# The order of every engine's instructions made by a second timing model, in a two-layer hybrid decoder trunk

## The chip, the cores and the metric

The kernel runs on one core of one Trainium2 chip. The metric is the device time of one launch, in microseconds (us). Engines are called as in the profile: PE is TensorE's matmul row, PEld its weight loads, DVE is VectorE, ACT is ScalarE, POOL is GpSimd, SP is SyncE, which issues all DMAs here.

## The reference

The reference computes two decoder layers on 256 rows of 1024 floats. Each layer norms its input, projects it, runs two groups of heads on the projection and puts their gated outputs through one output projection:

```python
for layer in range(DEPTH):
    h = rmsnorm(x, pre_norm[layer])
    proj = h @ w_in[layer]
    (hq, hf, hi, hz, nq, kc, vc, ks, vs, kw, vw, ng, nz) = jnp.split(proj, offsets, axis=-1)
    o_h = hgrn2_mixer(heads(hq), heads(hf), heads(hi), lower_bounds[layer].reshape(HGRN_HEADS, HEAD_DIM))
    o_h = rmsnorm(o_h, hgrn_out_norm[layer]).reshape(B, S, HGRN_WIDTH) * jax.nn.silu(hz)
    o_n = nsa_mixer(heads(nq), heads(kc), heads(vc), heads(ks), heads(vs), heads(kw), heads(vw), ng, ...)
    o_n = o_n.reshape(B, S, NSA_WIDTH) * jax.nn.silu(nz)
    y = jnp.concatenate([o_h, o_n], axis=-1).astype(x.dtype) @ w_out[layer]
    x = x + rmsnorm(y, post_norm[layer]).astype(x.dtype)
```

`hgrn2_mixer` is a gated linear recurrence with 8 heads of 128 by 128 state. `nsa_mixer` is attention with 8 query heads and three branches (compressed blocks, selected blocks, a sliding window), mixed by sigmoid gates. Everything is float32.

## The kernel before, in words

**Matmuls.** A float32 product is made of three products of parts: each operand is split into a high part of type fp32r and the rest. The normed input stands in SBUF as Hhi and Hlo for the whole layer. Projections are done in two shapes: `mm_a` (L363, matmuls L368 to L370) with the input stationary and 512 weight columns moving, and `mm_b` (L373, L378 to L380) with the weights stationary and 256 rows moving. The output projection is `mm_o` (L995, L997 to L999).

**Weights.** The list `plan` (L182) holds all weight units of both layers, 168 of them. `Ring.fill` (L206) issues their DMAs on SP into five raw buffers; `Ring.convert` (L199) splits each: ACT casts the high part (L202, whi) and DVE subtracts it for the low part (L203, wlo), into eight buffers each. A unit's buffers are given back when the matmuls that read it are done (`done`, L240).

**Planned order.** The kernel is traced in an order that its author writes by hand with a small clock: `tick` (L126) counts matmul time, `later` (L122) puts a piece of work some us behind, and `flush` (L131) forces it out. Transposes, rope, softmax steps, scans and conversions come between the projections' matmuls in this way. `norm_in` (L335) is the input norm: squares and sums on ACT (L339), a sum on DVE (L341), the root on ACT and its reciprocal on DVE (L331, L332), the scaling on DVE (L344), then `turn_h`: transposes on PE (L351) and their copies into Hhi on ACT (L355) and Hlo on DVE (L356). `finish` (L1002) is the post-norm of half of the rows, of the same kind (L1008 on ACT, L1009, L1010 and L1014 on DVE, and L331 and L332), and calls `norm_in` for the second layer. At the seam of the layers the chain is: last matmul of a half, L1008, L1009, L1010, L331, L332, L1014, L339, L341, L331, L332, L344, L351, L355, first L368.

**Attention.** For each half of the rows and each of two key groups: scores (L608 to L610), maximum and exp (L627 on DVE, L630 on ACT), coefficients and scaling (L640 to L651 on DVE), transposes (L668) with copies (L670 on ACT, L671 on DVE), values (L686 to L688), and a copy of the result (L691 on ACT). The compressed keys are roped at L386 to L393 and transposed at L531 (tile kst).

**Gates.** `hz` (L963) takes the gate projection from PSUM with a SiLU (L974) and multiplies (L978); `nz` (L439) does the same for attention (L450, L453). PSUM is shared out in banks: three with the tag mm for projections, two s, two t, one o.

**The framework's part.** What the kernel writes is not the final order. On leaving the TileContext, the framework runs the traced program through a timing model. Whenever an engine can take an instruction, the scheduler gives it, among those whose operands and buffers are ready in the model, the one that was traced first. So the traced order is a preference, and the model decides what is passed over. It then places the semaphores for the order that came out. On the chip each engine runs its instructions in that fixed order. This goes for PE, ACT, DVE, POOL and for SP's DMA issues, and also fixes which buffer of a pool a tile gets. A second, general path (`layers(True)`, L1120) is in the program behind a branch that is not taken with these inputs.

## Time and profile before

| | us |
|---|---|
| median of 3 runs | 566.41 |
| lowest and highest run | 566.41 and 568.52 |
| the profiled execution, its own time | 566.25 |
| its span, from the first to the last instruction | 564.5 |
| PE busy | 548.2 (97%) |
| DVE busy | 398.0 (71%) |
| ACT busy | 332.2 (59%) |
| mean granted clock of TensorE, as a share of full speed | 0.994 |

The profile is of one execution. Its span is 1.75 us shorter than the time of that execution; that part lies around the span. Busy time is the union of an engine's instructions. Matmuls are pipelined and overlap, so that a matmul's own duration (0.40 us for 512 columns) is longer than the distance to the next one. A row of a timeline gives the start in us from the span's start, the duration, engine, line, operation, output and inputs, shapes and number of instructions; in brackets stands how long the engine was idle before it and what ended that.

### The profile page before, as it was taken

What the parts mean: (1) busy time and instruction counts of PE and PEld (TensorE: products, weight loads), DVE (VectorE), ACT (ScalarE), POOL (GpSimd) and SP (SyncE); (2) the same over time, 40 slices, a digit from 0 to 9 for tenths busy, and PEclk for the clock granted to TensorE, in tenths of its full rate; (3) what the DMA queues carried; (4) which work ended last, traced back from release to release, by engine and by line L of the source; (5) the groups of instructions that cost most, each with busy time, mean ns of one, the idle gap of its engine ahead of it and who ended that gap; (6) DMA issues with size and microseconds to landing.
All of it is one profiled execution on the core that took longest, in us unless ns stands there. A gap on an engine that the chain in (4) does not pass through costs nothing. (4 is left out here: it accounts for less than half of the span.)

```text
span 564.5 us, 9581 instructions
## 1 busy us (share of the span) xinstructions
PE 548.2 (97%) x3563; PEld 490.3 (87%) x3563; DVE 398.0 (71%) x880; ACT 332.2 (59%) x626; POOL 9.6 (2%) x18
## 2 busy tenths in 40 slices
PE   7999999999999999999989999999999999999993
PEld 4889998999888989988878999879988898998882
DVE  4897997889577277663678599878967654866422
ACT  6577447855366785552557763686626768746310
POOL 4000000000000001001000000000000000000000
PEclk9999999999999999999999999999999999999997
DMA  8697559953146058565475755698423622856111
GB/s 302 204 315 236 150 149 280 302 175 114 38 126 194 21 186 291 162 214 151 133 240 170 230 151 157 197 303 257 117 72 82 170 87 70 301 172 202 40 38 43
DMA packets 72196, 96.55 MB, mean 171 GB/s; under 512 B 3383, under 2 KB 49229, under 8 KB 72142
## 3 DMA queue, kind: packets, MB, share of 16 engines
q1 hardware_dynamic: 72142, 95.86, 55.3%
q8 instruction: 30, 0.49, 0.3%
q14 instruction: 24, 0.20, 0.1%
HBM read 93.75 MB, written 2.10 MB: 170 GB/s over the span
## 5 line engine op out<-in xcount | busy, mean ns | idle before, releaser
L203 DVE TENSOR_TENSOR wlo<-raw,whi 128x1024 fp32r<-128x1024 f32 (+1 forms) x168 | 202.8, 1222 | 60.4 <-ACT whi L202 57.4
L202 ACT CAST whi<-raw 128x1024 fp32r<-128x1024 f32 (+1 forms) x168 | 175.0, 1052 | 89.0 <-PE ps_mm L379 24.4
L378 PE MATMUL ps_mm<-Hhi,whi 128*128 128x256 f32 x448 | 127.5, 285 | 0.0
L379 PE MATMUL ps_mm<-Hlo,whi 128*128 128x256 f32 x448 | 125.7, 281 | 0.0
L380 PE MATMUL ps_mm<-Hhi,wlo 128*128 128x256 f32 x448 | 125.7, 280 | 0.0
L368 PE MATMUL ps_mm<-whi,Hhi 128*128 128x512 f32 (+1 forms) x256 | 101.5, 397 | 2.3 <-ACT Hhi L355 2.3
L369 PE MATMUL ps_mm<-wlo,Hhi 128*128 128x512 f32 (+1 forms) x256 | 98.9, 386 | 0.0
L370 PE MATMUL ps_mm<-whi,Hlo 128*128 128x512 f32 (+1 forms) x256 | 98.8, 387 | 0.0
L379 PEld LDWEIGHTS ps_mm<-Hlo,whi 128*128 128x128 f32 x448 | 84.5, 189 | 0.1
L378 PEld LDWEIGHTS ps_mm<-Hhi,whi 128*128 128x128 f32 x448 | 84.3, 188 | 0.1
L380 PEld LDWEIGHTS ps_mm<-Hhi,wlo 128*128 128x128 f32 x448 | 84.4, 188 | 0.0
L368 PEld LDWEIGHTS ps_mm<-whi,Hhi 128*128 128x128 f32 x256 | 48.9, 191 | 10.2 <-ACT Hhi L355 3.0
L370 PEld LDWEIGHTS ps_mm<-whi,Hlo 128*128 128x128 f32 x256 | 48.6, 190 | 10.2 <-DVE Hlo L356 0.3
L369 PEld LDWEIGHTS ps_mm<-wlo,Hhi 128*128 128x128 f32 x256 | 48.8, 191 | 7.6 <-DVE wlo L203 0.5
L627 DVE CUSTOM_DVE_ANT_0 ps_s<-ps_s,cm 128x128 f32<-128x128 f32 (+1 forms) x64 | 22.4, 370 | 2.1 <-PE ps_s L610 0.7
L630 ACT ACTIVATE sB<-ps_s,nm 128x256 f32<-128x256 f32 (+1 forms) x40 | 16.9, 430 | 10.8 <-DVE nm L627 10.1
L671 DVE TENSOR_TENSOR sB<-ps_t,sB 128x512 fp32r<-128x512 f32 x12 | 8.2, 687 | 20.1 <-ACT sB L670 20.1
L1009 DVE TENSOR_TENSOR sA<-ps_mm,sB 128x512 f32<-128x512 f32 x6 | 4.2, 692 | 21.6 <-ACT st L1008 21.6
L997 PE MATMUL ps_mm<-whi,sN 128*128 128x512 f32 x48 | 19.0, 396 | 0.0
L998 PE MATMUL ps_mm<-wlo,Hhi 128*128 128x512 f32 x48 | 19.0, 395 | 0.0
L999 PE MATMUL ps_mm<-whi,Hlo 128*128 128x512 f32 x48 | 18.9, 395 | 0.0
L999 PE MATMUL ps_mm<-whi,sN 128*128 128x512 f32 x48 | 18.9, 394 | 0.0
(282 smaller groups left out, 927.7 us busy)
## 6 DMA issues: line engine op xcount, KB each, us to landing
raw<-in_w_in SPq DMA_DIRECT2D x112, 512.0 KB, 4.6
raw<-in_w_out SPq DMA_DIRECT2D x32, 512.0 KB, 4.3
raw<-in_w_in SPq DMA_DIRECT2D x8, 536.0 KB, 4.7
raw<-in_cmp_w_k SPq DMA_DIRECT2D x16, 256.0 KB, 3.3
raw<-in_cmp_w_v SPq DMA_DIRECT2D x16, 256.0 KB, 3.3
sB<-in_x SPq DMA_DIRECT2D x3, 512.0 KB, 3.5
sB<-in_post_norm SPq DMA_DIRECT2D x2, 512.0 KB, 5.4
xs<-sB SPq DMA_DIRECT2D x4, 256.0 KB
```

What stands on the lines that cost most here:

```text
L202: S.copy(out=hi, in_=raw)
L203: V.tensor_tensor(out=lo, in0=raw, in1=hi.bitcast(F32), op=OP.subtract)
L368: P.matmul(out=ps, lhsT=hh, rhs=wh, start=k == 0, stop=False)
L369: P.matmul(out=ps, lhsT=hh, rhs=wl, start=False, stop=False)
L370: P.matmul(out=ps, lhsT=hl, rhs=wh, start=False, stop=k == KT - 1)
L378: P.matmul(out=ps, lhsT=wh, rhs=hh, start=k == 0, stop=False)
L379: P.matmul(out=ps, lhsT=wh, rhs=hl, start=False, stop=False)
L380: P.matmul(out=ps, lhsT=wl, rhs=hh, start=False, stop=k == KT - 1)
L627: V.tensor_tensor_reduce(out=sb[b], in0=sb[b], in1=mk[b], scale=-1.0, scalar=3e38, op0=OP.add, op1=OP.min, accum_out=nm[:, i, b:b + 1])
L997: P.matmul(out=ps, lhsT=hi, rhs=wh, start=first, stop=False)
L998: P.matmul(out=ps, lhsT=hi, rhs=wl, start=False, stop=False)
L999: P.matmul(out=ps, lhsT=lo, rhs=wh, start=False, stop=last)
```

## The change

The context is told to use the framework's other timing model for the scheduling, a timeline simulation, instead of the default. No line of the computation changes, and the traced order stays as it was. The kernel has no other place that reads the flag.

```diff
-    with tile.TileContext(nc) as tc, ExitStack() as ctx:
+    with tile.TileContext(nc, schedule_with_timeline_sim=True) as tc, ExitStack() as ctx:
         build(ctx, tc, A, out)
```

## Rows read from the trace of the kernel before

**Rows 1.** Part 1 of the page: busy us, share of the span, instructions.

```profile
PE 548.2 (97%) x3563; PEld 490.3 (87%) x3563; DVE 398.0 (71%) x880; ACT 332.2 (59%) x626; POOL 9.6 (2%) x18
```

**Rows 2.** Waits of TensorE: line waited for, us in total, times, longest us.

```profile
PE ps_mm L1056 <- DMA sB<-in_pre_norm: 2.4, 1, 2.4
PE ps_mm L368 <- ACT Hhi L355: 2.3, 2, 1.8
PE ps_t L531 <- DVE kst L393: 1.3, 1, 1.3
PE ps_t L351 <- DVE sA L344: 1.0, 1, 1.0
```

**Rows 3.** Windows: stretch, busy us of PE, PEld, DVE, ACT, POOL; clock, DMA.

```profile
14.11:280.00 265.89, 265.80 (x1757) 239.84 (x1756) 195.84 (x440) 161.64 (x300) 3.67 (x3) 1.00 0.59 181
285.00:551.00 266.00, 264.73 (x1754) 239.05 (x1753) 189.24 (x420) 157.49 (x302) 0.00 (x0) 1.00 0.52 158
```

**Rows 4.** Timeline of PE, seam: start us, us, line, op, tiles, shape, idle before.

```profile
282.28 0.60 PE L351 MATMUL ps_t<-ct,sA 128*128 128x128 f32 x4
284.68 0.50 PE L368 MATMUL ps_mm<-whi,Hhi 128*128 128x512 f32 x1 [1.80 <-ACT Hhi L355]
...
285.71 0.40 PE L370 MATMUL ps_mm<-whi,Hlo 128*128 128x512 f32 x1
```

**Rows 5.** Timeline of DVE in the same stretch.

```profile
272.21 0.15 DVE L1010 TENSOR_TENSOR yss<-yss 128x1 f32<-128x1 f32 x1
273.30 1.23 DVE L203 TENSOR_TENSOR wlo<-raw,whi 128x1024 fp32r<-128x1024 f32 x1 [0.94 <-ACT whi L202]
274.45 0.16 DVE L332 RECIPROCAL r<-r 128x1 f32<-128x1 f32 x1
...
279.52 1.21 DVE L203 TENSOR_TENSOR wlo<-raw,whi 128x1024 fp32r<-128x1024 f32 x1
280.65 1.41 DVE L344 SCALAR_TENSOR_TENSOR sA<-sB,r,sB 128x512 f32<-128x512 f32 x2
```

**Rows 6.** Timeline of ACT in the same stretch.

```profile
273.18 0.29 ACT L331 ACTIVATE r<-yss,eps_t 128x1 f32<-128x1 f32 x1
...
282.52 1.04 ACT L202 CAST whi<-raw 128x1024 fp32r<-128x1024 f32 x1 [2.19 <-DMA raw<-in_w_in]
...
284.05 1.07 ACT L355 CAST Hhi<-ps_t 128x512 fp32r<-128x512 f32 x2
```

**Rows 7.** Part 5 of the page: weight split; busy us, mean ns, idle us before.

```profile
L203 DVE TENSOR_TENSOR wlo<-raw,whi 128x1024 fp32r<-128x1024 f32 (+1 forms) x168 | 202.8, 1222 | 60.4 <-ACT whi L202 57.4
L202 ACT CAST whi<-raw 128x1024 fp32r<-128x1024 f32 (+1 forms) x168 | 175.0, 1052 | 89.0 <-PE ps_mm L379 24.4
```

**Rows 8.** Timelines of DVE and PE, end of the first layer's attention.

```profile
204.66 0.69 DVE L671 TENSOR_TENSOR sB<-ps_t,sB 128x512 fp32r<-128x512 f32 x1
...
205.48 0.28 PE L686 MATMUL ps_o<-sB,vhi 128*128 128x256 f32 x1
```

**Rows 9.** Timeline of DVE before kst is ready, second layer.

```profile
371.59 3.50 DVE L203 TENSOR_TENSOR wlo<-raw,whi 128x1024 fp32r<-128x1024 f32 x3 [0.53 <-ACT whi L202]
...
375.44 0.21 DVE L393 TENSOR_TENSOR kst<-kst,rt 15x64 f32<-15x64 f32 x1
```

**Rows 10.** Waits of ACT for weight loads: us in total, times, longest us.

```profile
ACT whi L202 <- DMA raw<-in_w_in: 10.0, 10, 2.2
```

**Rows 11.** Timelines of ACT at a table load and of PE at the kernel's start.

```profile
197.01 1.28 ACT L943 ACT_TABLE_LOAD   x1
198.31 0.31 ACT L943 ACTIVATE hr<-hss,eps_t 128x16 f32<-128x16 f32 x1
...
12.43 0.63 PE L370 MATMUL ps_mm<-whi,Hlo 128*128 128x512 f32 x1
```

**Rows 12.** Timelines of ACT and PE: a bank emptied, and the group that takes it.

```profile
200.89 0.62 ACT L974 ACTIVATE sA<-ps_mm 128x512 f32<-128x512 f32 x1
...
207.94 0.48 PE L368 MATMUL ps_mm<-whi,Hhi 128*128 128x512 f32 x1
```

## Prediction

> **What bounds the kernel now.** I read four views in this order: the busy table, the waits of TensorE, the windows, and the timelines of the few places where TensorE stops. The busy table [rows 1] has TensorE at 548.2 of 564.5 us. The instructions stay what they are under the change, so only the remaining 16.3 us and the order can move. The waits [rows 2] name 7.0 us of those: 2.4 us before the first matmul (the first load), 1.0 us for the first norm, 2.3 us in front of L368 for Hhi, and 1.3 us in front of L531 for kst. The other 9.3 us are the tail after the last matmul. The windows [rows 3] say that the two long stretches between are full: 265.80 of 265.89 us and 264.73 of 266.00 us busy, at a granted clock of 1.00, the 2.4 GHz level. ScalarE and VectorE are busy 161.64 and 195.84 us in the first of them: they are not the bound, but everything that TensorE eats goes through them.
>
> So **a better order can gain only what stands in these waits**, and a worse one can lose as much as it takes away from the lead that ScalarE and VectorE have over TensorE.
>
> **Where the lead is thick.** The weights are split by L202 and L203, 168 times, 1052 and 1222 ns each [rows 7]. A ring holds 8 split units. 168 units feed 532 us of matmuls (the two stretches of [rows 3]), so one unit is 3.2 us of TensorE work and a full ring about 25 us. A conversion that is issued one or two places later is hidden by that stock. If the ring ran empty, each one would cost its 1.22 us.
>
> **Where it is thin: the seam of the two layers.** The last matmuls of the first layer are followed by L351 (transposes of the normed rows), L355 and the first L368 of the second layer. L351 starts its last group at 282.28 us and L368 follows at 284.68, after 1.80 us of idle [rows 4]. The chain to L351 changes engine at each step, and in each step it stands behind weight conversions. Sums of squares are added at 272.21 us (done 272.36), the root L331 starts at 273.18 on ScalarE [rows 5, 6], 0.8 us later. The reciprocal follows at 274.45, behind the conversion of 273.30: the root was done at 273.47, so 1.0 us more. L344 starts at 280.65, when the conversion of 279.52 is through. And L355, whose transposes were there at about 282.9 us, comes at 284.05, behind a conversion of 282.52: 1.1 us [rows 4, 6]. These delays are some 4 us, and part of them is hidden by the matmuls of the other half; 1.8 us reach TensorE. This is also the place that shows that the order is the framework's: the first L370 stands at 285.71, 1.03 us behind the first L368 and so some four matmuls later, where the program has it third of its group.
>
> **Thin hand-offs in attention.** The last VALUE step waits for L671: it runs from 204.66 to 205.35 us and L686 starts at 205.48, a lead of 0.13 us [rows 8]. And kst: its last step L393 came at 375.44 us, because three conversions from 371.59 on stood ahead of the rope [rows 9]; that is the 1.3 us of [rows 2].
>
> **The change part by part.** It removes and adds no operation. It moves any of them by the second model's opinion of what is ready. (1) TensorE's own order: matmuls cost the same at any place, so 0 by itself, if operands are there. (2) ScalarE and VectorE at the seam. The chain has six changes of engine. Bounds: −1.8 us (all conversions behind the chain) and +6.8 us (one conversion more at each of six, 6 × (1.05 + 1.22)/2). I take two more, one on each engine: 1.05 + 1.22 = +2.3 us, since at that place TensorE already waits and nothing covers them; two, because conversions become ready there about once per freed unit, as the six changes against one conversion each now show. (3) The hand-offs with 0.13 us of lead: a conversion ahead costs 1.22 − 0.13 = 1.1 us. Four places (two attention ends in each layer), bounds 0 and 4.4; I take two, +2.2 us. (4) kst: −1.3 us to +1.3 us (the first layer gets what the second has); I take 0. (5) DMA issues on SP: the weight loads stay in the order of the list, small loads can move past them. ScalarE waits for a weight load 10 times now, 2.2 us at most [rows 10]; the ring covers that, 0, with −0.5 to +2.2 as ends. POOL's memsets run far ahead of their readers: 0. (6) Table loads of ScalarE. One takes 1.28 us: it starts at 197.01 and its activation, the next instruction, at 198.31 [rows 11]. A new order of sigmoid, silu, exp and root could add some, between 0 and 1.3 us each; I take 0, since ScalarE idles for 40% of the time and none stands in the seam's chain. The Trainium skill (ScalarE: Activation LUTs, What ACT_TABLE_LOAD costs) counts a drain of about 1.38 us on top, 2.66 us per switch. The trace does not agree: the activation follows the load by 0.02 us [rows 11]. By the page, one extra switch in a chain would be 2.7 us and the sum would be 573.4 us.
>
> **The sum** is made against the profiled execution, 566.25 us (span 564.5 and 1.75 around it), which lies 0.16 us under the median of the runs, 566.41. 566.25 + 2.3 + 2.2 = 570.75, say **570.8 us**, 0.8% slower. A difference of about 0.5% (2.8 us) is what a measurement of this kernel can tell from no change; the three runs lie 0.4% apart.
>
> **Rivals.** *No change that can be told.* The second model is ready with nearly the same opinions, or gives the very same order; swaps stay inside the ring's 25 us and the seam stays as it is. For it: 97% busy, and the ring's stock. Against it: the seam and the four thin hand-offs have no cover at all. Time 566.2 to 568. Chance 0.33.
>
> *Faster: the seam and kst close.* If the second model sees the conversions become ready later than the norm's steps, L331, L332, L344 and L355 go ahead of them, and kst ahead of its three. Price: −1.8 − 1.3 = −3.1 us, 563.1 us. It decides when at most one of the six changes at the seam meets a conversion. For it: 4 us of conversions stand in that chain now, so there is something to take out. Against it: it needs both places, since either alone is below 0.5%. Nothing larger is to be had, as [rows 2, 3] show. Chance 0.21.
>
> *Much slower: the gate's PSUM banks come free late.* Projections rotate over three banks (tag "mm"). In the gate stage a bank is emptied by the SiLU L974, which stands behind squares, root and two table loads on ScalarE; it empties the second of two at 200.89 to 201.51 us, and the next group, which needs one of them, starts at 207.94 [rows 12], a lead of at least 6.4 us. It decides from there: if the new order puts over 6.4 us of ready conversions and copies ahead of that chain, TensorE stops, since it issues in order. A slip of 10 us (eight or nine conversions) gives 3.6 us in each layer, 7.2 in all, on top of the forecast: 578.0 us. For it: an order by readiness has no notion of a chain that is late. Against it: 6.4 us is a long way, and ScalarE idles 40% of the time. Chance 0.10.
>
> What a longer stop could cost besides: a 512-column matmul at the start of the kernel takes 0.63 us [rows 11], after the seam 0.40 [rows 4]. So the 1.80 us of the seam did not take the clock to its lower level, and a stop of that size costs nothing beyond itself here. The Trainium skill (TensorE: Matmul & The Clock Gate, Part 1) says that an idle array falls back to 1.2 GHz and has to be busy again before it gets 2.4 GHz. No row here shows that inside the kernel; by it a stop much longer than the seam's would add 0.23 us to each of some matmuls behind it: 2.3 us for ten, 573.1 us in all, inside the range.
>
> **How the numbers follow.** Forecast 0.36, much slower 0.10, no change 0.33, faster 0.21. Faster by over 0.5%: 0.21. Within: 0.33. Slower: 0.36 + 0.10 = 0.46. Cases of both signs hold much of the chance, so the forecast's own range is 568.5 (one of the items) to 577 (all of (2) and (3)). The range for all is 562.5 to 580: below it lies the end of the faster case (about 0.10), above it the longer slips of the much slower one (about 0.08).
>
> **What would show it.** Right: the wait of L368 for Hhi at the seam grows from 1.8 to about 4 us, with L331, L332 or L355 directly behind L202 or L203; new waits of TensorE of about 1 us in front of L686 or L668 behind L671 and L651. No change: the same four waits within 0.5 us. Faster: the waits in front of L368 and L531 are gone and no others appear. Much slower: waits of several us in front of L368 in the gate stage, near 208 and 481 us, for L974. I am wrong altogether if TensorE's busy time itself grows while its waits don't, or if the head (before the first L368) or the tail moves by more than 1 us: there I count nothing, since the head is the first load and the tail a chain of data without conversions.

## The result and the profile after

The changed kernel takes **583.18 us** (median of 4 runs, 582.66 to 585.32) against 566.41 us for the kernel before: a ratio of 1.0287, 95% interval 1.0253 to 1.0322. It is 16.8 us slower, above the range that was forecast (562.5 to 580.0). The profiled execution has a span of 580.9 us, 16.4 more than before. The busy table of its page, which answers to [rows 1]:

```profile
PE 553.8 (95%) x3563; PEld 493.5 (85%) x3563; DVE 398.7 (69%) x880; ACT 333.6 (57%) x626; POOL 9.6 (2%) x18
```

The instructions are the same in number on every engine. TensorE's busy time grew by 5.6 us and its idle time by 10.8. The waits of TensorE (line waited for, us in total, times, longest us), which answer to [rows 2]:

```profile
PE ps_mm L368 <- ACT sA L974: 5.7, 2, 2.8
PE ps_t L351 <- DVE sA L344: 3.3, 2, 2.3
PE ps_mm L1056 <- DMA sB<-in_pre_norm: 2.3, 1, 2.3
PE ps_s L853 <- ACT sB L630: 1.6, 2, 0.8
PE ps_o L681 <- ACT pcT L659: 1.5, 2, 0.8
PE ps_mm L368 <- ACT Hhi L355: 1.2, 2, 0.7
PE ps_s L608 <- ACT sB L630: 1.0, 2, 0.5
PE ps_s L934 <- ACT sB L630: 0.7, 2, 0.4
```

The largest is new: TensorE stops in front of L368 for L974, the gate's SiLU, once in each layer. The wait for kst is gone. Four small waits on the softmax's ScalarE steps (L630, L659) are new.

The next two fences show one source line each over 110 to 250 us (the first layer): first of the kernel before, then of the changed one. The two times behind the colon are the first and the last start.

```profile
L608 PE MATMUL ps_s<-kTh,q x24: 279/291/392, 113.3 to 180.5; 128*128 128x272 f32 x16, 128*128 128x256 f32 x8
L934 PE MATMUL ps_s<-sA,ATt x32: 271/275/275, 183.1 to 194.3; 128*128 128x128 f32 x32
L974 ACT ACTIVATE sA<-ps_mm x4: 594/600/616, 199.9 to 214.3; 128x512 f32<-128x512 f32 x4
```

```profile
L608 PE MATMUL ps_s<-kTh,q x24: 279/287/384, 112.8 to 196.5; 128*128 128x272 f32 x16, 128*128 128x256 f32 x8
L934 PE MATMUL ps_s<-sA,ATt x32: 275/275/377, 197.4 to 203.5; 128*128 128x128 f32 x32
L974 ACT ACTIVATE sA<-ps_mm x4: 589/596/601, 210.5 to 221.0; 128x512 f32<-128x512 f32 x4
```

The scores (L608) begin within 0.5 us of each other, and the last one starts 16.0 us later. The last mix (L934) starts 9.2 us later, the first SiLU 10.6 us later. What fills TensorE in between can be read from windows of 10 us (columns as in [rows 3]). First two of the kernel before, then the same two of the changed one and the two where it pays:

```profile
120.00:130.00 10.00, 10.00 (x82) 9.81 (x83) 9.73 (x37) 5.36 (x16) 0.00 (x0) 1.00 0.34 104
130.00:140.00 10.00, 10.00 (x85) 9.48 (x84) 9.40 (x27) 6.16 (x17) 0.00 (x0) 1.00 0.55 158
```

```profile
120.00:130.00 10.00, 10.00 (x86) 10.00 (x85) 9.55 (x34) 5.04 (x14) 0.00 (x0) 1.00 0.69 195
130.00:140.00 10.00, 10.00 (x54) 8.41 (x53) 6.81 (x17) 4.60 (x11) 0.00 (x0) 1.00 0.42 123
200.00:210.00 10.00, 7.61 (x66) 7.13 (x64) 4.22 (x13) 9.92 (x38) 0.00 (x0) 1.00 0.19 59
210.00:220.00 10.00, 8.82 (x40) 7.40 (x41) 6.99 (x16) 6.48 (x10) 0.00 (x0) 0.83 0.27 77
```

From 130 to 140 us TensorE is full in both kernels, but with 54 instructions instead of 85: long projections in place of short attention steps. Nothing is lost there. The bill comes at 200: the projections that can go ahead are through, three banks are full, and only the late, dependent steps are left. Now ScalarE is the engine that is full (9.92 of 10), and then the granted clock falls to 0.83. The stop itself, on ScalarE and on TensorE (timelines):

```profile
207.01 0.59 ACT L670 CAST sB<-ps_t 128x512 fp32r<-128x512 f32 x1
207.62 1.28 ACT L943 ACT_TABLE_LOAD   x1
208.91 0.31 ACT L943 ACTIVATE hr<-hss,eps_t 128x16 f32<-128x16 f32 x1
209.24 1.28 ACT L974 ACT_TABLE_LOAD   x1
210.53 1.09 ACT L974 ACTIVATE sA<-ps_mm 128x512 f32<-128x512 f32 x2
```

```profile
211.18 0.50 PE L368 MATMUL ps_mm<-whi,Hhi 128*128 128x512 f32 x1 [2.83 <-ACT sA L974]
211.52 0.39 PE L369 MATMUL ps_mm<-wlo,Hhi 128*128 128x512 f32 x1
...
212.38 0.63 PE L369 MATMUL ps_mm<-wlo,Hhi 128*128 128x512 f32 x1
212.81 0.63 PE L370 MATMUL ps_mm<-whi,Hlo 128*128 128x512 f32 x1
```

The matmul of 512 columns takes 0.63 us at the 1.2 GHz level and 0.39 us at 2.4, and starts follow at 0.43 and 0.23 us. In the first layer 8 starts from 211.99 to 215.37 us stand at the lower level (3.38 us where 8 × 0.233 = 1.87 would do), in the second 14 from 492.75 to 498.83 (6.08 instead of 3.27): 1.5 + 2.8 = 4.3 us. They count as busy, so most of TensorE's 5.6 us of added busy time is the same work at half speed.

**The account of the profiled execution**: stops 2 × 2.83 = 5.7, half speed 4.3, the four small waits of attention 4.8, the seam +1.6 (idle 2.28 + 0.47 + 0.68 = 3.4 us against 1.80), kst −1.3. Together 15.1 of 16.4 us.

### The profile page after: what moved, and what is told of

Read it like the earlier page. It is cut to its first block, busy times and chain, and to the rows that moved or that the text cites. A ratio compares the mean times of both kernels' runs of the same rounds, so it can differ in the third digit from the quotient of the medians.

```text
span 580.9 us, 9606 instructions
## 1 busy us (share of the span) xinstructions
PE 553.8 (95%) x3563; PEld 493.5 (85%) x3563; DVE 398.7 (69%) x880; ACT 333.6 (57%) x626; POOL 9.6 (2%) x18
## 5 line engine op out<-in xcount | busy, mean ns | idle before, releaser
L203 DVE TENSOR_TENSOR wlo<-raw,whi 128x1024 fp32r<-128x1024 f32 (+1 forms) x168 | 203.6, 1223 | 81.6 <-ACT whi L202 78.1
L368 PE MATMUL ps_mm<-whi,Hhi 128*128 128x512 f32 (+1 forms) x256 | 101.9, 398 | 6.9 <-ACT sA L974 5.7
L370 PE MATMUL ps_mm<-whi,Hlo 128*128 128x512 f32 (+1 forms) x256 | 100.1, 392 | 0.7 <-DVE Hlo L356 0.7
L369 PE MATMUL ps_mm<-wlo,Hhi 128*128 128x512 f32 (+1 forms) x256 | 100.4, 393 | 0.0
L368 PEld LDWEIGHTS ps_mm<-whi,Hhi 128*128 128x128 f32 x256 | 49.6, 194 | 17.1 <-ACT sA L974 6.1
L370 PEld LDWEIGHTS ps_mm<-whi,Hlo 128*128 128x128 f32 x256 | 49.7, 194 | 10.5 <-DVE Hlo L356 1.4
L630 ACT ACTIVATE sB<-ps_s,nm 128x256 f32<-128x256 f32 (+1 forms) x40 | 17.1, 430 | 25.1 <-DVE nm L627 17.1
L997 PE MATMUL ps_mm<-whi,sN 128*128 128x512 f32 x48 | 19.0, 395 | 0.0
L998 PE MATMUL ps_mm<-wlo,sN 128*128 128x512 f32 x48 | 18.9, 394 | 0.0
L999 PE MATMUL ps_mm<-whi,Hlo 128*128 128x512 f32 x48 | 18.7, 396 | 0.0
L997 PE MATMUL ps_mm<-whi,Hhi 128*128 128x512 f32 x48 | 18.6, 395 | 0.0
L630 ACT ACTIVATE sN<-ps_s,nm 128x128 f32<-128x128 f32 (+1 forms) x24 | 9.4, 400 | 15.9 <-DVE nm L627 13.5
```

What stands on the lines that cost most here:

```text
L203: V.tensor_tensor(out=lo, in0=raw, in1=hi.bitcast(F32), op=OP.subtract)
L368: P.matmul(out=ps, lhsT=hh, rhs=wh, start=k == 0, stop=False)
L369: P.matmul(out=ps, lhsT=hh, rhs=wl, start=False, stop=False)
L370: P.matmul(out=ps, lhsT=hl, rhs=wh, start=False, stop=k == KT - 1)
L630: S.activation(out=Pm[i][:, b, :], in_=sb[b], func=AF.Exp, bias=nm[:, i, b:b + 1], scale=-1.0, accum_out=sm[:, i, 1 + b:2 + b])
L997: P.matmul(out=ps, lhsT=hi, rhs=wh, start=first, stop=False)
```

## The experiments

The order that a model makes can be taken out of it and tied to the instructions of the other: an edge from each instruction of an engine to the next, which sets the order of issue and makes nothing wait for a result. The model then only orders what is left free, and it orders that anew, around the tied engine. All orders below are stored as runs of positions in the listed program. Line numbers in these kernels are shifted by the lists. In the first model's order 281 of TensorE's 3417 instructions stand elsewhere than in the list, in the second model's 1509.

```diff
+    def put_in_order(engine, runs):
+        seq = [i for i in nc.cur_bb.bb.instructions if i.engine == engine ...]
+        seq = [seq[s + k] for s, n in runs for k in range(n)]
+        for p, i in zip(seq, seq[1:]):
+            tc.add_manual_dep(i, p.name, mybir.DependencyInfo(mybir.DependencyClass.NoSync,
+                              mybir.DependencyReason.DATA), reason="order")
...
     layers(False)
+    put_in_order(mybir.EngineType.PE, RUNS)
```

### TensorE's order against all the others

The kernel before, with TensorE in the second model's order (the edit above, RUNS from the changed kernel):

> The first model schedules, but TensorE's 3417 matmuls and transposes are tied in the order that the second model gave them; ScalarE, VectorE and the queues stay with the first model. Theory A (the 16.8 us come from TensorE's own order: projections issued ahead of attention, then a stop for the gate's PSUM banks): 580 to 585 us, with the two stops of about 3 us in front of L368 for L974. Theory B (they come from the orders of ScalarE and VectorE, conversions ahead of the softmax): 566 to 571 us.

Measured: 581.37 us, ratio 1.0261 [1.0233, 1.0288]. TensorE waits 5.8 us in front of the gate's projections for the SiLU, as in the changed kernel. The changed kernel, with TensorE in the first model's order:

> The second model schedules, but TensorE's 3417 instructions are tied in the order that the first model gave them. Theory A: 564 to 569 us, no wait of L368 for L974 over 0.5 us, and the kst wait may stay closed (then nearer to 564). Theory B: 579 to 584 us.

Measured: 583.61 us, ratio 1.0329 [1.0290, 1.0368]. **Each theory was right in one run and wrong in the other.** Tying the second model's order of TensorE to the kernel before costs 15.2 us, and tying the first model's to the changed kernel leaves 17.5, where the flag costs 16.8. In the second run there is no stop for the gate; the time goes in small waits inside attention and in 3.0 us at the seam. Its VectorE and TensorE, timelines (the conversion L203 is L217 here, the scaling L651 is L665, the transposes L668 are L682):

```profile
125.70 0.22 DVE L650 TENSOR_TENSOR pc<-pc,cm 128x64 f32<-128x64 f32 x1
126.46 1.23 DVE L217 TENSOR_TENSOR wlo<-raw,whi 128x1024 fp32r<-128x1024 f32 x1 [0.54 <-ACT whi L216]
...
129.35 1.22 DVE L217 TENSOR_TENSOR wlo<-raw,whi 128x1024 fp32r<-128x1024 f32 x1
...
131.09 0.87 DVE L665 TENSOR_SCALAR sN<-sN,sm 128x128 f32<-128x128 f32 x4
```

```profile
131.43 0.94 PE L682 MATMUL ps_t<-ct,sN 128*128 128x128 f32 x4 [1.50 <-DVE sN L665]
```

Two conversions stand between the steps of one softmax, where the kernel before has one, in a stretch where VectorE is full (9.41 us of 120 to 130), and TensorE waits for the result. In the changed kernel TensorE has projections in that stretch (the windows above).

These two runs don't split the loss into halves, since the free engines follow the tied one. By the places of the same instructions in the traces, VectorE's stand in the first run 1.5 places on average from the changed kernel's order and 3.8 from the order before, ScalarE's 0.3 and 3.9; in the second run it is the other way round, with 2.2 places from the order before and 3.6 from the changed kernel's on VectorE, 0.4 and 3.9 on ScalarE. So the first run shows that TensorE's order, with what the first model then does to the others, is enough for the stops and for most of the loss. The second shows that moves on VectorE and ScalarE that are small by comparison cost as much when TensorE keeps the first model's order.

**The listed order.** Two runs tied TensorE in the order of the list, under the second and under the first model (the edit is the one above with the runs left out):

> The second model schedules, TensorE's instructions are tied in the order in which the program lists them. In the first model's order 281 of 3417 stand elsewhere than in the list, in the second's 1509. Theory A: 564 to 570 us, near the tied order of the first model. Theory B: 579 to 584 us.

> Control of the run before: the first model, TensorE's instructions tied in the listed order. Theory A: 565 to 570 us, within 2 us of the same order under the second model. Theory B: also 565 to 570 us, but 10 us or more below the second model with the same order. If the few moves that the first model makes on TensorE are worth something, this one is slower than the kernel before by what they are worth.

Measured: 610.78 us (1.0789 [1.0759, 1.0819]) and 598.81 us (1.0574 [1.0546, 1.0601]). The times that both theories named were far off. The 281 moves of the first model are worth 33 us: without them TensorE waits 17.2 us for L344 and 7.9 us for a constant's load (prow). The idea that the first model's order is good because it is near the list was wrong; few moves in the right places make it good.

### Which of the other engines

A ladder down from the second run above: TensorE tied in the first model's order, and one engine more tied at each step.

> The second model, with TensorE's and VectorE's instructions tied in the first model's orders; 81 of ScalarE's instructions and 26 of SP's loads stand elsewhere than before. Theory C (VectorE's order is the other half: the weights' second conversions L203 stand ahead of softmax steps and wait there for ScalarE's first half, with the softmax queued behind them): 564 to 569 us. Rival S (ScalarE's or SP's moves cost it): 575 us or more.

> The second model with TensorE, VectorE and ScalarE all tied in the first model's orders; 26 of SP's 215 loads and two memsets of GpSimd still stand elsewhere. Against the run with TensorE and VectorE tied (576.3 us) only ScalarE's 81 places are new. If those 81 places cost the 10.5 us that were left: 565 to 569 us. If SP's loads cost them: 574 to 578 us.

> The second model with TensorE, VectorE, ScalarE and also SP's 215 loads tied in the first model's orders; two memsets of GpSimd change places and the order in which semaphores are numbered differs. If order is all that the flag changes, and the 4.8 us left were SP's loads: 564 to 567 us. If the 4.8 us come from anything else: about 570 us.

Measured: 576.28 us (1.0187 [1.0142, 1.0233]), 570.23 us (1.0090 [1.0071, 1.0109]), 566.16 us (0.9995 [0.9970, 1.0020]). Each set of runs has its own times of the kernel before; above these the four runs of the ladder lie by 17.5, 10.5, 4.8 and 0.4 us. So, with TensorE's order kept, VectorE's costs 7.0 us, ScalarE's 81 displaced instructions 5.7, SP's 26 displaced loads 4.4, each to within some 2 to 3 us by the intervals, and nothing is left: **order is all that the flag changes.** Theory C, which had VectorE alone as the other half, was wrong in its "564 to 569"; the run of 570 us lies between its two expectations. What SP's order costs shows in part in the waits of TensorE in the run of 570 us: it waits 2.0 us for prow (a constant, loaded in two parts of 32 KB), and for kst in both layers (1.3 us of that stand in the kernel before too):

```profile
PE ps_t L623 <- DVE kst L485: 2.1, 2, 1.5
PE ps_t L385 <- DMA prow<-in_cmp_pos_v: 2.0, 1, 2.0
```

Between the profiles of these last two runs (spans 568.5 and 563.2 us) TensorE's idle time differs by 2.8 us and its busy time by 2.5. Part of the latter are matmuls at the lower clock behind the wait for prow (the last section has the rows).

Two mixtures left TensorE and ScalarE free and tied VectorE alone:

> The first model, with VectorE alone tied in the second model's order; TensorE and ScalarE are ordered freely around it (TensorE then stands 4.4 places per instruction from the second model's order and 11.3 from the first's). Theory C: 578 to 585 us, and the stop of L368 for L974 comes back. Rival (VectorE's order hurts only where TensorE's is held fast, as in the second run of the first set): 566 to 571 us.

> The second model, with VectorE alone tied in the first model's order; TensorE and ScalarE are ordered freely. Theory C with VectorE as the root: 564 to 571 us. Rival (TensorE's order of the second model is bad by itself, whatever VectorE does): 578 to 585 us, with the stop for L974.

Measured: 599.75 us (1.0574 [1.0535, 1.0614]) and 593.95 us (1.0480 [1.0433, 1.0528]). Both are worse than either kernel and lie above every time that was expected. The second was expected at 564 to 571 if VectorE were the root: it is not. In these two runs a model that is forced to one engine's order of the other model makes a worse whole than either model does alone.

### Where in the program

The first model's orders on TensorE, VectorE and ScalarE, tied only for what is listed from the start of attention to the end of the second gate, and the counterpart with everything else tied:

```diff
+            mark()
             flush("q")
             attention(PW, PS)
...
             nz(ring)
+            mark()
```

> The second model, with the first model's orders on TensorE, VectorE and ScalarE only for what is listed from the start of attention to the end of the second gate, in both layers; head, first projections, keys, output projection and seam are free. Theory L (the loss is made in that stage: the first output projection comes 7.0 us late, the seam adds 1.4, the second layer 8.2): 566 to 571 us, with no wait for L974. Rival (the orders of the stages are bound to each other, and a cut between two models costs waits of its own): 575 us or more.

> The counterpart: first model's orders for everything outside that stage, the second model inside it. Theory L: 579 to 585 us, with the two stops of about 3 us in front of L368 for L974. Rival: no more than half of the loss, 566 to 575 us.

Measured: 569.60 us (1.0078 [1.0053, 1.0104]) and 584.81 us (1.0359 [1.0332, 1.0387]). Theory L holds: the stage from attention to the gates, left to the second model, costs all of it; with that stage put right 4.2 us are left above the kernel before of the same set (565.45 us), so 12.6 of 16.8 us are back. The rest lies mainly at the seam, where this run waits longest, and with it the clock (timeline of TensorE; the matmuls behind the wait take 0.63 us again):

```profile
285.61 1.32 PE L450 MATMUL ps_t<-ct,sA 128*128 128x128 f32 x8 [3.28 <-DVE sA L443]
287.41 0.63 PE L467 MATMUL ps_mm<-whi,Hhi 128*128 128x512 f32 x1 [0.48 <-ACT Hhi L454]
287.84 0.63 PE L468 MATMUL ps_mm<-wlo,Hhi 128*128 128x512 f32 x1
```

### The stop at the gate: cause or symptom

First, only what is listed while the gate's projections are listed is held to its place of the first order, on TensorE alone:

```diff
+            mark()
             hz(l, ring, rs)
+            mark()
```

> The second model, with only TensorE's instructions listed while the gate's projections are listed (in hz) each held behind the instruction that stands ahead of it in the first model's order; ScalarE and VectorE are free, and so is the rest of TensorE. Theory G (the gate's projections run ahead, fill the three banks, and TensorE then has nothing but dependent steps until L974): the stop goes, and with it the half-speed matmuls behind it, 568 to 575 us. Rival (attention is late because of VectorE and ScalarE, the projections only fill time that would be waits): 579 us or more, with the stop replaced by waits in front of the scores, the mixes or the values.

Measured: 584.38 us (1.0342 [1.0319, 1.0364]). Theory G falls. The stop for L974 is gone, and waits for attention stand in its place (waits of TensorE; L608 is L631 here, L658 is L681):

```profile
PE ps_s L631 <- ACT sB L653: 3.9, 8, 0.7
PE ps_t L681 <- DVE pcs L671: 2.0, 2, 1.0
```

The half speed is not gone either. TensorE idles 2.5 us less than in the changed kernel (24.6 and 27.1 us) and is busy 4.3 us longer (558.1 and 553.8) with the same instructions; from 180 to 185 us, inside attention, the granted clock is 0.50.

Second, the SiLU is freed from the squares. Both write the buffer A2, so the SiLU cannot empty a bank before the last squares are done:

```diff
-        sq = slot("A2")
+        sq = small([128, 512], "sq", 1)
```

> The second model as in the changed kernel, with one buffer more: the squares of hgrn_o (L938) go to a tile of their own instead of the one that the gate's SiLU (L974) writes, so that the SiLU can empty the projection banks as soon as the projections are done. Theory G (the late attention costs what it does because the gate's banks cannot be emptied before it is through): the stops of 2.99 us and the half-speed matmuls behind them go, about 2 x 5 us, 571 to 576 us. Rival D (attention is late and everything behind it waits for it wherever the banks are): the stop moves to another place of the gate or the output projection, 580 us or more.

Measured: 578.79 us (1.0218 [1.0186, 1.0251]), between the two expectations. The stop for L974 is gone, about 4 us are won (13.0 us above the kernel before of its set, where the changed kernel is 16.8), and the waits go on into the last values of attention (waits of TensorE):

```profile
PE ps_o L687 <- DVE sB L671: 3.3, 4, 1.3
PE ps_t L351 <- DVE sA L344: 3.2, 2, 2.4
PE ps_o L686 <- ACT sB L670: 2.3, 4, 0.9
```

ScalarE also loads its tables eight times more (634 instructions instead of 626), since SiLU and exp now alternate. So the shared buffer makes the stop, but the stop is only one of the forms in which this stage loses its time. How late attention ends does not measure the loss (starts in the first layer, us):

| | last scores, L608 | last values, L686 | first output projection, L997 |
|---|---|---|---|
| kernel before | 180.5 | 205.8 | 237.3 |
| changed kernel | 196.5 | 219.4 | 244.3 |
| gate's projections held | 188.7 | 214.1 | 245.5 |
| squares in a buffer of their own | 200.1 | 222.8 | 243.2 |

Held back, the projections let attention end 5 to 8 us earlier than in the changed kernel, and the output projection still begins 8.2 us later than before. So the early projections of the gate seem mostly to fill time that would be waits, and attention is late without them as well.

### A kernel faster than both

The prediction's faster rival said that the seam and kst could be closed for 3.1 us. The kernel before, with the orders of TensorE, VectorE and ScalarE tied (three, where the expectation says four) and with hand-made changes of the lists in these two places, and with the one for kst alone:

> The kernel before, its four orders tied, with two places changed by hand. At the seam 16 instructions of VectorE and 13 of ScalarE: root, reciprocals, L339, L344, L355 and L356 ahead of the weight conversions there, and the eight transposes L351 some 1.9 and 1.8 us of matmuls earlier. At kst: L531 behind five more L493 in both layers. The prediction priced the two at 1.8 + 1.3 = 3.1 us: 563 us, ratio 0.994 to 0.996. Rival: the conversions held back make the first matmuls of the second layer wait for their weights instead, 565 to 567 us.

> The kernel before with its orders tied and only L531 moved behind five more L493, in both layers, on TensorE alone. The wait for kst goes (1.3 us and 0.25 us): 564.6 to 565.0 us against 566. If the steps behind L531 (L541, the scores) are late then, nothing is gained.

Measured: **563.77 us** (0.9960 [0.9944, 0.9975]) and 565.13 us (0.9991 [0.9973, 1.0009], which cannot be told from no change). The first is faster than both kernels, by a little: 0.4%, with an interval that leaves out 1. Its span is 561.5 us, 3.0 less than that of before; the medians differ by 2.0. At the seam the first L368 follows the output projection directly (timeline of TensorE; L997 to L999 are L1089 to L1091, L368 is L460):

```profile
281.78 0.40 PE L1091 MATMUL ps_o<-whi,Hlo 128*128 128x512 f32 x1
282.01 0.39 PE L460 MATMUL ps_mm<-whi,Hhi 128*128 128x512 f32 x1
```

### Conversions off VectorE

If the conversions are in the way on VectorE, another engine could have them:

```diff
-                V.tensor_tensor(out=lo, in0=raw, in1=hi.bitcast(F32), op=OP.subtract)
+                nc.gpsimd.tensor_tensor(out=lo, in0=raw, in1=hi.bitcast(F32), op=OP.subtract)
```

> The kernel before, with the second half of each weight conversion (L203, 168 times) on GpSimd instead of VectorE, so that no softmax step stands behind one. Theory C: no slower than before if GpSimd takes under about 3.2 us for one (TensorE's work per unit), 562 to 568 us; if it takes longer than that, GpSimd becomes the bound and the time is 168 times its duration.

Measured: 669.23 us, ratio 1.1811 [1.1769, 1.1852]. GpSimd takes 2.45 us for one, under the 3.2 us that were named, and still 103 us are lost. VectorE without the conversions had 398.0 − 202.8 = 195.2 us of work in the kernel before; here it is busy for 381.6 us, and the six longest waits of TensorE are all for VectorE. What lies behind that is in the last section.

## Why the prediction was wrong

**Step (1) failed**: TensorE's own order at 0, "if operands are there". Tying nothing but this order to the kernel before costs 15.2 us. Operands are there for each matmul that is put ahead: TensorE stays full of projections while the steps with a long chain behind them move back, and the condition is broken some 70 us later. I priced the move of each instruction where it stands, not what the moved work does to the end of the chain behind it, nor what the other engines' orders become around it.

The terms, as predicted and as the changed kernel's profile has them:

| term | predicted us | measured us |
|---|---|---|
| (1) TensorE's order: stops at the gate | 0 (rival: 7.2) | 5.7 |
| clock behind the stops | 0 (aside: 2.3 for ten matmuls) | 4.3 |
| (2) seam | +2.3 | +1.6 |
| (3) hand-offs in attention | +2.2 | +4.8 |
| (4) kst | 0 | −1.3 |
| (6) table loads | 0 | 0 (626 instructions as before) |

(2) was right in kind and nearly in size: L331 comes behind two conversions, L332 behind two and L344 behind one. (3) was right that thin hand-offs grow, and wrong in place: L671 in front of L686 makes no wait at all; the four are behind the exp (L630), which frees the two score banks, and the copy L659. (4) went to its lower bound. (5) SP at 0 holds within the changed kernel, where no wait for prow shows; under the first model's orders on the other engines the same loads cost 4.4 us.

**The much slower rival was the mechanism, and its chance of 0.10 was the mistake.** It named the place (L368 in front of L974, near 208 and 481 us; it is 211 and 493), a slip of 10 us (measured 10.6) and a stop of 3.6 us per layer (2.83). Two arguments stood against it. "6.4 us is a long way": but what slips is not a few conversions in front of the SiLU, it is attention itself, 16.0 us at the last scores and 13.6 at the last values. "ScalarE idles 40% of the time": an average over the kernel; from 200 to 210 us, where the stop begins, it is busy for 9.92 of 10. The same trap is in the reading of [rows 3], from which I called VectorE not the bound (195.84 of 265.89 us): from 120 to 140 us of the kernel before it is busy 9.73 and 9.40 of 10, and just there the softmax steps are chosen against conversions. Its total of 578.0 lacks the clock and carries 2.2 instead of 4.8 us for the hand-offs; with these it would have been at 585. Even so its stop is not the whole of the loss: closed alone, in the run with the squares' own buffer, it gave back about 4 us.

The Trainium skill (TensorE: Matmul & The Clock Gate, Part 1) was quoted for a fall to 1.2 GHz behind a longer stop. The traces agree: 2.83 us of idle time in each layer are followed by 22 matmuls at the lower level in all, where the aside had taken ten; not every stop of two to three us is followed by any (last section). The prediction's own sentence, that a stop of 1.80 us costs nothing beyond itself, holds for the kernel before only: in the run with the second model's order of TensorE, matmuls at 0.63 us follow a seam's stop of 1.77 us.

The bound on the other side held: what the faster rival could win was put at 3.1 us, and 2.0 were won by hand.

**What stays open.** Which of the moved steps makes attention late is not shown: with the gate's projections in their old places the time stayed at 584.4 us, and no run held the other engines to the changed kernel's whole orders while TensorE alone was moved. Why the second model ranks the projections ahead can't be read from a trace of the chip: its opinions of durations don't stand there. VectorE's order with the first model's order on both TensorE and ScalarE was not tried, so its 7.0 us are known only in that place of the ladder. In the run with the squares' own buffer the eight added table loads (8 × 1.28 us on ScalarE) are not separated from the rest.

## What to carry to other kernels

A change of order alone, with the same instructions, moved this kernel between 564 and 611 us; so "the busiest engine is 97% full" bounds what a new order can win and says nothing about what it can lose. Before you call an engine not the bound, read its windows where the chains run (ten-microsecond windows, not the average), and follow the longest chain to the resource that it frees: work that is put ahead can fill that resource and then wait for the chain. The orders of the engines belong together: the four kernels here with one engine tied to the other model's order took 581 to 600 us, against 566 for the kernel before. Keep a good schedule whole and improve single places.

## What the runs showed of the hardware that was not expected

**GpSimd holds up VectorE.** In the run with the conversions on GpSimd, VectorE's own instructions grow. Two groups of that run by line and form (busy us, mean ns; L390 reads PSUM and one SBUF tile, L393 two SBUF tiles), and two rows of its VectorE timeline:

```profile
L390 DVE TENSOR_TENSOR rt<-ps_mm,ct 128x64 f32<-128x64 f32 x8 | 1.8, 226 | 9.4 <-ACT kst L386 9.4
L393 DVE TENSOR_TENSOR kst<-kst,rt 128x64 f32<-128x64 f32 x8 | 37.9, 4735 | 0.2
```

```profile
66.02 2.42 DVE L774 TENSOR_TENSOR gc<-ce,fs 128x16 f32<-128x16 f32 x1
68.37 2.54 DVE L775 COPY gc<-ce 128x16 f32<-128x16 f32 x1
```

In the kernel before the groups take 223 and 224 ns: L390 is untouched, L393 is 21 times as long on average, and unevenly: over the ten L393 on kst the median is 1.34 us, the longest 18.26. And L774 and L775, on 16 elements, last 2.42 and 2.54 us each (0.18 and 0.17 before), the length of one GpSimd conversion (2.45 us): they stand in a stretch in which GpSimd runs six conversions in a row. The Trainium skill (SBUF — State Buffer, Who interferes with whom) says that a VectorE instruction with two SBUF inputs, or a copy in a two-port mode, shares a pair of ports with GpSimd, and that the loser waits for the whole instruction of the other. The traces agree for the instruction with two SBUF inputs; that L775, a copy, ran in such a mode is not shown, only that it was held up for as long. The longest L393 runs from 443.75 to 462.01 us, and GpSimd runs ten conversions in a row from 438.49 to 461.92: here VectorE got through only when the row was over, not after one instruction of the other.

**The clock behind a stop.** In the changed kernel three matmuls behind the first layer's stop still ran at the 2.4 GHz level before eight ran at 1.2; behind the second layer's, 14 at 1.2 GHz came at once, and the granted clock of 490 to 500 us was 0.66. The length of a stop does not tell by itself whether the clock falls. Stops of 1.80 us ([rows 4]) and of 2.28 us (the changed kernel's seam) left it where it was, and so did one of 2.61 us in the run with TensorE and VectorE tied, while matmuls at 1.2 GHz came behind 2.04 us in the run of 570 us (timelines of TensorE, L368 to L370 are L430 to L432 and L460 to L462):

```profile
290.25 0.50 PE L430 MATMUL ps_mm<-whi,Hhi 128*128 128x512 f32 x1 [2.61 <-ACT Hhi L417]
290.59 0.39 PE L431 MATMUL ps_mm<-wlo,Hhi 128*128 128x512 f32 x1
```

```profile
29.54 0.30 PE L385 MATMUL ps_t<-ct,prow 128*128 128x128 f32 x1 [2.04 <-DMA prow<-in_cmp_pos_v]
...
31.21 0.63 PE L462 MATMUL ps_mm<-whi,Hlo 128*128 128x512 f32 x1
```

In the run with the gate's projections held, the clock fell behind four waits of 0.33 to 0.70 us between 173 and 178.5 us, with no other wait in the 17 us before these.
